# Matmul with RMS norm: the first pair of contraction tiles loaded through the software DMA queue, with its rows spread over the partitions

## Chip, cores and metric

The kernel runs on one core of one Trainium2 chip. The metric is the device time of one execution in microseconds. Before the change it is 222.75 us, the median of 7 runs (222.26 to 223.61). Work on the core is done by TensorE (matmuls and transposes; PE in the profile, its weight loads PEld), VectorE (DVE), ScalarE (ACT), GpSimd (POOL) and SyncE (SP). Loads and stores are issued by SP and ACT (two hardware queues) or by GpSimd (the software queue, which can also cast f32 to bf16 on the way), and all run on the core's 16 DMA engines.

## What is computed

```python
def setup_inputs():
    m, k, n = 2048, 2048, 2048
    return {
        "a": np.random.randn(m, k).astype(np.float32),
        "b": np.random.randn(k, n).astype(np.float32),
        "gamma": np.random.randn(n).astype(np.float32),
        "eps": np.float32(1e-5),
    }

def reference(a, b, gamma, eps):
    x = np.matmul(a, b)
    rms = np.sqrt(np.mean(x ** 2, axis=-1, keepdims=True) + eps)
    return (gamma * x / rms).astype(np.float32)
```

## The kernel before

A is cut into 16 blocks of 128 rows, the contraction into 16 tiles of 128 (KT), taken as 8 pairs (KP, index `kp`), and the columns of B into two halves (index `j`) of 1024, each two chunks of 512 (CH). TensorE needs both operands with the contraction on the partitions. B lies so in memory; A must be transposed. Whichever row of B lies on a partition, the same column of A must lie there in the transposed A: the order inside a contraction tile is free, as long as both agree.

**The head**, some 57 us, works while A and B stream in. The first four blocks of A (HB, 512 rows) are loaded pair by pair as pieces of 512 rows by 256 columns, and B's left half (j = 0) as tiles of 256 rows by 1024 columns, both cast to bf16 by the software queue (`load_head`, with the A load on L105 and the B load, `load_b`, on L99). TensorE transposes the A piece of the next pair (`transpose_head`, L172; VectorE moves the result to `head_at`, L177) and multiplies (`stream`, L384, seven accumulators in PSUM; the eighth group goes through `stream_in_parts`, L415, and VectorE's addition L421). Meanwhile VectorE forms sums and differences of quarters of B (`b_sums` L275, `b_sums_in_place` L280), since all later products use a two-by-two scheme with seven products instead of eight. Then B's right half (j = 1) streams in with its products for the first four blocks.

**The first pair** (kp = 0) goes another way, so as to start early. A's piece (512 rows by 256 columns, 0.5 MB) is loaded as f32 by SP (L91) into `a0f`, and B's two tiles of 128 rows by 1024 columns as f32 by ACT (L93) into `b0f`. `transpose_first` transposes A as f32 (L155), VectorE moves it to `head_at` as bf16 (L161), and VectorE and ScalarE cast B's halves into `raw[0][0]` (L158, L160). Until then TensorE runs eleven matmuls on zeros (L145) to keep its clock up. The identity for the transposes is made by GpSimd (a memset and a select), between its first and its second pair of loads, and VectorE casts it to bf16 and f16 (L138, L140).

**After the head** the other twelve blocks are taken in pairs (`group_half`, two halves each; `last_group` for the last pair). A block is loaded whole as f32 (two blocks by halves, L115, ten whole, L120), its row norms are taken on ScalarE (`row_norm`, L223), and `row_apply` scales the rows by a power of two and casts them to f16: on VectorE for blocks 4 and 5 (L244), on ScalarE for the others (L246). Blocks 4 and 5 are transposed on TensorE (`turn`, `transpose_half`, L189), the others by a DMA transpose from SP (L199). Sums of A's quarters (`a_sums`, L264), seven products (L289), and the combination on VectorE and ScalarE follow.

The order is written out by hand: `tc.manual_schedule()` puts each instruction on its engine's queue in the order of the program text, and every engine works its queue in that order. GpSimd's queue holds loads 1 to 3 of the pairs, the identity between them, small memsets, and then a load each time one that was issued eight loads earlier has landed.

The slots in SBUF that the change touches are parts of `early`:

```python
    a0f = early[:, 0:2048].bitcast(FP32).rearrange("p (r k) -> p r k", r=HB)
    b0f = [early[:, 2048 + t * 2048:2048 + (t + 1) * 2048].bitcast(FP32) for t in range(2)]
```

Of the kernel before, what the change touches and what calls it, by code (L numbers as in the profile page):

```python
# [8 lines left out]
FP32 = mybir.dt.float32  # L9
BF16 = mybir.dt.bfloat16  # L10
FP16 = mybir.dt.float16
I32 = mybir.dt.int32
ACTF = mybir.ActivationFunctionType
# [4 lines left out]
def kernel(  # L18
# [13 lines left out]
    nc = tc.nc  # L32
    P = 128
# [4 lines left out]
    W2 = 2 * P  # L38
    MB = M // P
    CH = 512  # L40
    NCH = N // CH
    HALF = N // 2
    HB = 4
# [15 lines left out]
    early = consts.tile([P, 6 * 2048], BF16, name="early")  # L59
    head_at = consts.tile([P, KT, HB, P], BF16, name="head_at")  # L60
    raw = [[consts.tile([P, 2, HALF], BF16, name=f"b_{j}_{kp}") for kp in range(KP)]
           for j in range(2)]
# [2 lines left out]
    sums = [t_left, t_right]  # L65

    a0f = early[:, 0:2048].bitcast(FP32).rearrange("p (r k) -> p r k", r=HB)
    b0f = [early[:, 2048 + t * 2048:2048 + (t + 1) * 2048].bitcast(FP32) for t in range(2)]
    NAH = 6
    ah_slot = [early[:, 6144 + s * 1024:6144 + (s + 1) * 1024].rearrange("p (r k) -> p r k", r=HB)  # L70
               for s in range(NAH)]
# [9 lines left out]
    def a16_slot(mb):  # L81
        flat = head_at.rearrange("p t r m -> p (t r m)").bitcast(FP16)
        return flat[:, (2 + mb % 2) * K:(3 + mb % 2) * K]
# [4 lines left out]
        return (at_even, at_odd)[(mb // 2) % 2][:, mb % 2]  # L88


    nc.sync.dma_start(out=a0f, in_=a[0:HB * P, 0:W2].rearrange("(r p) k -> p r k", p=P))  # L91
    for t in range(2):
        nc.scalar.dma_start(out=b0f[t], in_=b[t * P:(t + 1) * P, 0:HALF])  # L93

    def ah(kp):
        return ah_slot[(kp - 1) % NAH]

    def load_b(j, kp):
        nc.gpsimd.dma_start(  # L99
            out=raw[j][kp],  # L100
            in_=b[kp * W2:(kp + 1) * W2, j * HALF:(j + 1) * HALF].rearrange(
                "(t p) n -> p t n", p=P))

    def load_head(kp):
        nc.gpsimd.dma_start(  # L105
            out=ah(kp),
            in_=a[0:HB * P, kp * W2:(kp + 1) * W2].rearrange("(r p) k -> p r k", p=P))
        load_b(0, kp)

    a32 = {}  # L110
# [13 lines left out]
    def wait_for(src):  # L124

        nc.gpsimd.tensor_copy(out=pace, in_=src)

    load_head(1)
    identity_f = t_left[:, 2, KP - 1, 0:2 * P].bitcast(FP32)
    make_identity(nc, identity_f)  # L130
# [6 lines left out]
    identity = consts.tile([P, P], BF16, name="identity")  # L137
# [11 lines left out]

    def transpose_first():  # L150
        bank = [ps_t.tile([P, CH], FP32, name="tbank"), ps_a.tile([P, CH], FP32, name="acc")]
        view = [b.rearrange("p (r m) -> p r m", r=HB) for b in bank]
        for t in range(2):
            for r in range(HB):
                nc.tensor.matmul(view[t][:, r, :], a0f[:, r, t * P:(t + 1) * P], identity_f,  # L155
                                 is_transpose=True, start=(r == 0), stop=(r == HB - 1))
        for t in range(2):
            cast_first = [lambda: nc.vector.tensor_copy(out=raw[0][0][:, t, :CH],  # L158
                                                        in_=b0f[t][:, :CH]),
                          lambda: nc.scalar.copy(out=raw[0][0][:, t, CH:], in_=b0f[t][:, CH:])]  # L160
            move = [lambda h=h: nc.vector.tensor_copy(  # L161
                out=head_at[:, t, 2 * h:2 * h + 2, :], in_=view[t][:, 2 * h:2 * h + 2, :])
                for h in range(2)]
            for work in (cast_first + move if t == 0 else move + cast_first):
                work()

    def transpose_head(kp):
        bank = ps_t.tile([P, CH], FP32, name="tbank")
# [10 lines left out]
    a16 = {}  # L179
# [36 lines left out]
    factor = {}  # L216
# [22 lines left out]

    def row_apply(mb):  # L240
        a16[mb] = a16_slot(mb)
        if mb < HB + 2:

            nc.vector.tensor_scalar_mul(out=a16[mb], in0=a32.pop(mb), scalar1=factor.pop(mb))  # L244
        else:
            nc.scalar.activation(out=a16[mb], in_=a32.pop(mb), func=ACTF.Copy,  # L246
                                 scale=factor.pop(mb))


    def quarter(g, r, c):  # L250
# [141 lines left out]
    def load_later(n):  # L392
        for _ in range(min(n, len(later))):
            kind, which = later.pop(0)
            load_b(1, which) if kind == "b" else load_half(HB + which // 2, which % 2)
# [36 lines left out]
    for r in range(HB):  # L432
        x_tile(r, 0)
    early_sums = {4: ((2,), 0, 6), 5: ((5,), 0, 7), 6: ((1,), 0, KP)}
    transpose_first()
    for kp in range(KP):
        if kp + 4 < KP:
# [81 lines left out]
    row_factor(HB)  # L519
    product(PAIR, 1, 3, pair[5], start=False)  # L520
    row_apply(HB)
    nc.scalar.copy(out=x21, in_=pair[2])
    row_factor(HB + 1)
    row_apply(HB + 1)
    p7 = new_bank()
    turned = {}
# [88 lines left out]
    def hooks_of(g, j):  # L615
# [8 lines left out]
        def apply(mb):  # L624
            row_apply(mb)
            transpose_dma(mb)
# [204 lines left out]
```

## Time and profile before

| what | value |
|---|---|
| median of 7 runs | 222.75 us |
| the profiled execution, in all | 223.17 us |
| its span, first to last instruction | 221.4 us |
| TensorE busy | 208.9 us (94% of the span) |
| VectorE busy | 167.7 us (76%) |
| ScalarE busy | 128.3 us (58%) |
| GpSimd busy | 29.4 us (13%) |
| mean granted TensorE clock | 0.989 |
| read from HBM, written to it | 34.60 MB, 16.78 MB |
| first product on real data (L384) | 7.55 us |
| last B tile's first use | 56.85 us |

The profile is one execution taken by the hardware profiler. A row of the busy shares has 40 slices of 5.5 us, each digit the share in tenths. The chain of work that ended last is followed back from the last instruction, at each step to what released it. In a timeline line stand the start, the duration, the engine, the line of the program, the operation, what it writes and reads, and in brackets how long the engine had been idle before it and what ended that. "Time to landing" of a DMA runs from its issue to its completion as the engines see it. Rates of DMA count the bytes written, so a load that casts f32 to bf16 reads twice what the rate says.

### The profile page before, as it was taken

The page shows a single profiled execution, that of the slowest core. Times are in us where ns is not written, and L with a number is a line of the kernel's source. Part 1 is how long each engine was busy: PE and PEld are TensorE (multiplying, and loading weights), DVE is VectorE, ACT ScalarE, POOL GpSimd, SP SyncE. Part 2 cuts the span into 40 slices and gives each one's busy share as a digit, 9 for nine tenths or more (in the row PEclk, how much of TensorE's full clock was granted, in tenths as well). Part 3 has the DMA queues.
Part 4 walks back from the last instruction along what each step waited for, and adds up shares of the span by engine and source line. Part 5 has one row for each costly group of instructions (what it writes and reads, how often), then busy time and mean ns, then how long its engine had stood idle before and what let it go on. Part 6 is the DMA issues. An engine that isn't in the chain of part 4 may idle for free.

```text
span 221.4 us, 3002 instructions
## 1 busy us (share of the span) xinstructions
PE 208.9 (94%) x1015; PEld 97.7 (44%) x1035; DVE 167.7 (76%) x330; ACT 128.3 (58%) x263; POOL 29.4 (13%) x59
## 2 busy tenths in 40 slices
PE   7899999999999999999999999999999999999950
PEld 2445444444455444444444444444444444444430
DVE  2428889999988898989695639855794759797691
ACT  3110002920598898778845997399738995334580
POOL 7634232210000001200200002000200000000040
PEclk9999999999999999999999999999999999999995
DMA  6999999999938496947899049955798349044045
GB/s 185 226 201 209 204 207 211 212 210 241 421 111 355 181 298 110 372 184 203 213 313 406 16 88 267 369 219 95 183 298 374 69 90 380 33 189 192 1 191 189
DMA packets 36320, 47.13 MB, mean 213 GB/s; under 512 B 21968, under 2 KB 26064, under 8 KB 34896
## 3 DMA queue, kind: packets, MB, share of 16 engines
q0 software_dynamic: 9936, 23.33, 41.3%
q1 hardware_dynamic: 25936, 22.29, 33.4%
q10 hardware_dynamic: 432, 1.31, 1.9%
q8 instruction: 8, 0.13, 0.2%
q14 instruction: 8, 0.07, 0.1%
HBM read 34.60 MB, written 16.78 MB: 232 GB/s over the span
## 4 chain that ended last, share of the span: by engine, by line
PE 68%; DMA 23%; DVE 2%; POOL 2%; issue 2%; ACT 1%; DVEq 0%; ACTq 0%; POOLq 0%
PE acc L289 66%; DMA b<-in_b_dram 23%; POOL early L105 1%; DVE x L709 1%; PE acc L384 1%; POOL b L99 1%; DVE x L712 1%; ACT sq L307 0%; PE tbank L189 0%; PE acc L189 0%; DVE a L709 0%; ACT sq L778 0%; DVE x L786 0%; DVEq L826 0%; DVE x L790 0%
## 5 line engine op out<-in xcount | busy, mean ns | idle before, releaser
L289 PE MATMUL acc<-b,s 128*128 128x512 bf16 x397 | 91.5, 379 | 1.1 <-DMA b<-in_b_dram 0.5
L289 PEld LDWEIGHTS <-s 128*128 128x128 f16 (+1 forms) x512 | 49.9, 98 | 60.6 <-issue 0.8
L384 PE MATMUL acc<-b,head_at 128*128 128x512 bf16 x171 | 41.3, 379 | 0.7 <-DMA b<-in_b_dram 0.4
L307 ACT ACTIVATE sq<-x 128x512 bf16<-128x512 f32 x54 | 34.1, 632 | 6.9 <-DVE x L709 3.0
L366 DVE SCALAR_TENSOR_TENSOR x<-x,r,gamma_sb 128x1024 f32<-128x1024 f32 x28 | 34.8, 1281 | 0.7
L223 ACT ACTIVATE sq<-a 128x1024 bf16<-128x1024 f32 x24 | 25.3, 1055 | 1.8 <-DMA a<-in_a_dram 1.4
L384 PEld LDWEIGHTS <-head_at 128*128 128x128 bf16 x176 | 16.8, 98 | 20.2 <-issue 1.4
L246 ACT ACTIVATE head_at<-a,s 128x2048 f16<-128x2048 f32 x10 | 20.0, 1999 | 3.7 <-DVE s L233 3.7
L426 ACT COPY x<-acc 128x512 f32<-128x512 f32 x6 | 3.4, 588 | 25.1 <-PE acc L384 25.1
L289 PEld LDWEIGHTS <-head_at 128*128 128x128 f16 (+1 forms) x112 | 11.0, 98 | 13.2
L289 PE MATMUL acc<-early,head_at 128*128 128x512 bf16 x63 | 14.4, 379 | 0.1
L289 PEld LDWEIGHTS <-at_even 128*128 128x128 f16 x96 | 9.4, 98 | 11.3
L289 PE MATMUL acc<-early,s 128*128 128x512 bf16 x55 | 14.2, 379 | 0.0
L264 DVE TENSOR_TENSOR s<-head_at 128x1024 f16<-128x1024 f16 (+5 forms) x22 | 13.4, 638 | 0.1
L596 DVE TENSOR_TENSOR x<-x,x 128x512 f32<-128x512 f32 x9 | 6.2, 693 | 8.8 <-ACT x L594 8.3
L99 POOL DMA_DIRECT2D b<-in_b_dram x15 | 10.6, 707 | 15.4 <-DMA b<-in_b_dram 12.9
L578 ACT COPY x<-acc 128x512 f32<-128x512 f32 x9 | 5.2, 574 | 11.5 <-PE acc L289 11.5
L289 PE MATMUL acc<-t_left,s 128*128 128x512 bf16 x47 | 11.3, 379 | 0.1
L280 DVE TENSOR_TENSOR b<-b 128x1024 bf16<-128x1024 bf16 x16 | 10.9, 693 | 0.2
L289 PE MATMUL acc<-early,at_even 128*128 128x512 bf16 x48 | 10.8, 379 | 0.1
L289 PE MATMUL acc<-t_left,head_at 128*128 128x512 bf16 x48 | 10.8, 379 | 0.0
L289 PE MATMUL acc<-t_left,at_even 128*128 128x512 bf16 x47 | 10.8, 379 | 0.1
(111 smaller groups left out, 217.1 us busy)
## 6 DMA issues: line engine op xcount, KB each, us to landing
out_dram<-x SPq DMA_DIRECT2D x30, 512.0 KB, 3.8
a<-in_a_dram POOLq DMA_DIRECT2D x10, 1024.0 KB, 8.3
b<-in_b_dram POOLq DMA_DIRECT2D x15, 512.0 KB, 17.0
a<-in_a_dram POOLq DMA_DIRECT2D x4, 512.0 KB, 17.6
early<-in_a_dram POOLq DMA_DIRECT2D x7, 256.0 KB, 14.6
early<-in_b_dram ACTq DMA_DIRECT2D x2, 512.0 KB, 5.9
gamma_sb<-in_gamma_dram POOLq DMA_DIRECT2D x1, 1024.0 KB, 15.4
early<-in_a_dram SPq DMA_DIRECT2D x1, 512.0 KB, 5.5
```

Of the source, the lines that this page charges most:

```text
L99: nc.gpsimd.dma_start(out=raw[j][kp], in_=b[kp * W2:(kp + 1) * W2, j * HALF:(j + 1) * HALF].rearrange("(t p) n -> p t n", p=P))
L223: nc.scalar.activation(out=junk, in_=a32[mb][:, h * HALF:(h + 1) * HALF], func=ACTF.Square, scale=2.0 ** -8, accum_out=n2[:, h:h + 1])
L246: nc.scalar.activation(out=a16[mb], in_=a32.pop(mb), func=ACTF.Copy, scale=factor.pop(mb))
L264: nc.vector.tensor_tensor(out=sum_of(g, s)[:, lo:hi, :], in0=x[:, lo:hi, :], in1=y[:, lo:hi, :], op=op)
L280: nc.vector.tensor_tensor(out=flat[:, 1:3, :], in0=flat[:, 1:3, :], in1=flat[:, 0::3, :], op=ALU.add)
L289: nc.tensor.matmul(bank, lhsT[:, kp, :], rhs, start=(start and kp == 0), stop=(kp == KP - 1), skip_group_check=not start)
L307: nc.scalar.activation(out=sq[:, 0:CH], in_=src, func=ACTF.Square, scale=inv_sqrt_n, accum_out=msq[mb][:, c:c + 1])
L366: nc.vector.scalar_tensor_tensor(out=x, in0=x, scalar=inverse_of[mb], in1=gamma_sb[:, h * HALF:(h + 1) * HALF], op0=ALU.mult, op1=ALU.mult)
L384: nc.tensor.matmul(bank, head_at[:, kt, r, :], head_rhs(c, kt), start=(kt == 0), stop=(kt == KT - 1))
L426: copy(out=x_chunk(*g), in_=banks[g])
L578: nc.scalar.copy(out=c, in_=one[1])
L596: nc.vector.tensor_tensor(out=t, in0=t, in1=x12, op=ALU.add)
```

## The change

The first pair of contraction tiles is loaded, laid out and transposed in another way:

- B's rows of the first pair come by the software queue, cast to bf16 on the way and straight into `raw[j][0]`, as two loads of 128 rows for each half j (`load_first_pair`). For j = 0 they are the queue's first two loads. Row 32 v + u of a tile goes to partition 4 u + v, so neighbouring partitions hold rows 32 apart.
- A's 512-row piece of that pair is loaded by halves of 256 rows, one from SP and one from ACT.
- A's columns of that pair have to be permuted alike. VectorE and ScalarE cast two 128-row blocks each from `a0f` to a bf16 copy `a0`, reading with a stride of 32 elements; TensorE transposes the copy in bf16, and each of the two engines moves its half to `head_at`.
- For the blocks after the head, `row_apply` writes the first 256 columns permuted and the other 1792 as before: two instructions where there was one.
- Casts of B by VectorE and ScalarE and the f32 transposes go.

```diff
-    b0f = [early[:, 2048 + t * 2048:2048 + (t + 1) * 2048].bitcast(FP32) for t in range(2)]
+    a0 = early[:, 2048:3072].rearrange("p (r k) -> p r k", r=HB)
...
-    nc.sync.dma_start(out=a0f, in_=a[0:HB * P, 0:W2].rearrange("(r p) k -> p r k", p=P))
-    for t in range(2):
-        nc.scalar.dma_start(out=b0f[t], in_=b[t * P:(t + 1) * P, 0:HALF])
+    def spread_columns(cols):
+        return cols.rearrange("p (t v u) -> p t u v", v=4, u=P // 4)
+
+    def load_first_pair(j, t):
+        nc.gpsimd.dma_start(
+            out=raw[j][0][:, t, :],
+            in_=b[t * P:(t + 1) * P, j * HALF:(j + 1) * HALF].rearrange("(v u) n -> u v n", v=4))
+
+    for h, queue in enumerate((nc.sync, nc.scalar)):
+        queue.dma_start(out=a0f[:, 2 * h:2 * h + 2, :],
+                        in_=a[2 * h * P:(2 * h + 2) * P, 0:W2].rearrange("(r p) k -> p r k", p=P))
...
     def load_b(j, kp):
+        if kp == 0:
+            for t in range(2):
+                load_first_pair(j, t)
+            return
...
+    for t in range(2):
+        load_first_pair(0, t)
     load_head(1)
...
     def transpose_first():
         bank = [ps_t.tile([P, CH], FP32, name="tbank"), ps_a.tile([P, CH], FP32, name="acc")]
-        view = [b.rearrange("p (r m) -> p r m", r=HB) for b in bank]
-        for t in range(2):
-            for r in range(HB):
-                nc.tensor.matmul(view[t][:, r, :], a0f[:, r, t * P:(t + 1) * P], identity_f,
-                                 is_transpose=True, start=(r == 0), stop=(r == HB - 1))
-        for t in range(2):
-            cast_first = [lambda: nc.vector.tensor_copy(out=raw[0][0][:, t, :CH],
-                                                        in_=b0f[t][:, :CH]),
-                          lambda: nc.scalar.copy(out=raw[0][0][:, t, CH:], in_=b0f[t][:, CH:])]
-            move = [lambda h=h: nc.vector.tensor_copy(
-                out=head_at[:, t, 2 * h:2 * h + 2, :], in_=view[t][:, 2 * h:2 * h + 2, :])
-                for h in range(2)]
-            for work in (cast_first + move if t == 0 else move + cast_first):
-                work()
+        copies = (nc.vector.tensor_copy, nc.scalar.copy)
+        for h, copy in enumerate(copies):
+            for r in (2 * h, 2 * h + 1):
+                copy(out=a0[:, r, :].rearrange("p (t u v) -> p t u v", v=4, u=P // 4),
+                     in_=spread_columns(a0f[:, r, :]))
+        for h, copy in enumerate(copies):
+            view = bank[h].bitcast(BF16)[:, 0:CH].rearrange("p (t r m) -> p t r m", t=2, r=2)
+            for t in range(2):
+                for r in range(2):
+                    nc.tensor.matmul(view[:, t, r, :], a0[:, 2 * h + r, t * P:(t + 1) * P],
+                                     identity, is_transpose=True,
+                                     start=(t == 0 and r == 0), stop=(t == 1 and r == 1))
+            copy(out=head_at[:, 0:2, 2 * h:2 * h + 2, :], in_=view)
...
-        if mb < HB + 2:
-            nc.vector.tensor_scalar_mul(out=a16[mb], in0=a32.pop(mb), scalar1=factor.pop(mb))
-        else:
-            nc.scalar.activation(out=a16[mb], in_=a32.pop(mb), func=ACTF.Copy,
-                                 scale=factor.pop(mb))
+        x, s = a32.pop(mb), factor.pop(mb)
+        first = a16[mb][:, 0:W2].rearrange("p (t u v) -> p t u v", v=4, u=P // 4)
+        for dst, src in ((first, spread_columns(x[:, 0:W2])), (a16[mb][:, W2:], x[:, W2:])):
+            if mb < HB + 2:
+                nc.vector.tensor_scalar_mul(out=dst, in0=src, scalar1=s)
+            else:
+                nc.scalar.activation(out=dst, in_=src, func=ACTF.Copy, scale=s)
```

## The prediction, made before the changed kernel was built

> **What bounds the kernel now.** I read the page first: busy shares by slice, then the chain of work that ended last.
>
> ```profile
> PE   7899999999999999999999999999999999999950
> DMA  6999999999938496947899049955798349044045
> PE 68%; DMA 23%; DVE 2%; POOL 2%; issue 2%; ACT 1%; DVEq 0%; ACTq 0%; POOLq 0%
> PE acc L289 66%; DMA b<-in_b_dram 23%; POOL early L105 1%; DVE x L709 1%; PE acc L384 1%; POOL b L99 1%; DVE x L712 1%; ACT sq L307 0%; PE tbank L189 0%; PE acc L189 0%; DVE a L709 0%; ACT sq L778 0%; DVE x L786 0%; DVEq L826 0%; DVE x L790 0%
> ```
>
> TensorE looks full everywhere, but the chain says that up to about 57 us it is the loads of B (23% of the span) that end last, and after that matmuls in one unbroken run. The list of TensorE's waits up to 62 us shows how thin the difference is:
>
> ```profile
> PE acc L289 <- DMA b<-in_b_dram: 0.5, 1, 0.5
> PE acc L384 <- DMA b<-in_b_dram: 0.4, 1, 0.4
> PE tbank L415 <- DVE head_at L177: 0.3, 1, 0.3
> ```
>
> TensorE waits 0.4 us for a B tile at 24.5 us and 0.5 us for the last one at 56.85 us. So in the head two streams run side by side at one speed. The change works on the first 8 us of both; what counts is when the last B tile lands, and this follows from how early the software queue's stream gets going. The timeline of GpSimd gives its pace, because from its ninth load on GpSimd issues one load each time an older one lands:
>
> ```profile
> 1.25 0.94 POOL L105 DMA_DIRECT2D early<-in_a_dram  x1 [0.80 <-POOLq L812]
> 12.53 0.70 POOL L99 DMA_DIRECT2D b<-in_b_dram  x1 [1.76 <-DMA b<-in_b_dram]
> 16.32 0.70 POOL L99 DMA_DIRECT2D b<-in_b_dram  x1 [1.72 <-DMA b<-in_b_dram]
> 36.26 0.70 POOL L99 DMA_DIRECT2D b<-in_b_dram  x1 [1.76 <-DMA b<-in_b_dram]
> 38.73 0.57 POOL L115 DMA_DIRECT2D a<-in_a_dram  x1 [1.78 <-DMA b<-in_b_dram]
> 41.22 0.54 POOL L115 DMA_DIRECT2D a<-in_a_dram  x1 [1.92 <-DMA b<-in_b_dram]
> ```
>
> From 12.53 to 36.26 us six pairs (A tile 0.5 MB, B tile 1 MB) pass: 3.95 us a pair. 38.73 to 41.22 is one B tile: 2.5 us, which leaves 1.45 us for an A tile. The first B tile of this queue (issued at 2.18, time to landing 10.1 us) lands at 12.28 us. Taking off 2.5 and 1.45, the stream runs as if it had started at full pace at 8.32 us, though its first load was issued at 1.25 us. The windows show what filled the gap (columns: window, its length, busy time of PE, PEld, DVE, ACT, POOL, granted clock, DMA share, GB/s written):
>
> ```profile
> 2.50:3.00 0.50, 0.50 (x2) 0.15 (x1) 0.00 (x0) 0.49 (x2) 0.50 (x2) 1.00 0.86 176
> 4.00:4.50 0.50, 0.50 (x3) 0.22 (x2) 0.00 (x0) 0.00 (x0) 0.50 (x2) 1.00 1.01 383
> 6.00:6.50 0.50, 0.10 (x1) 0.13 (x2) 0.00 (x0) 0.00 (x0) 0.50 (x6) 1.00 0.78 214
> 8.00:8.50 0.50, 0.50 (x4) 0.26 (x3) 0.49 (x2) 0.00 (x0) 0.10 (x1) 1.00 1.42 203
> ```
>
> 383 GB/s written is f32 copied as f32 by the two hardware queues; about 205 at a share over 1.1 is the casting stream (it reads twice what it writes), and it reaches that only at 8 us. The three hardware loads land at 5.1 (B rows 0-127), 6.2 (A) and 8.7 us (B rows 128-255).
>
> **The change, part by part.** (1) *Bytes.* B's first pair (1 MB) goes from the ACT queue to the head of the software queue; A's 0.5 MB is split between SP and ACT. The new stream needs 2.5 + 1.45 + 2.5 = 6.45 us up to the landing of that same B tile. If it gets to full pace at S, the tile lands at S + 6.45, against 12.28: **break-even is S = 5.83 us**. Everything behind is the same stream at the same pace, so the last B tile moves by as much.
>
> How early can S be? No row shows this queue starting with little beside it at the beginning of the program, so I bound it. Early end: a 1 MB load of this queue that met idle DMA (L120, issued at 86.57) took 5.3 us to land; 2.5 of that is the stream, so 2.8 is start-up and S = 1.25 + 2.8 = 4.05. Late end: the queue needs the first 6.0 to 6.5 us whatever lies beside it, and S is 6.4. Which is nearer? The same 1 MB load took 8.4, 8.2 and 8.3 us at 109.6, 134.6 and 158.7 us, where SP's stores and transposes were running: 3 us more, so hardware-queue work ahead does hold this queue's start back. The first A load of the queue, 0.5 MB beside 1.5 MB of hardware loads, took 8.5 us. In the windows the casting stream appears when A's load is over (6.2 us). With 0.5 MB on the hardware queues, A is over earlier: 0.03 MB by 2.0 us, 0.27 MB by 3.5 us at the rates of those windows, the rest at 380 GB/s by 4.1 us, 0.4 us later for the landing. I take S = 4.7 (A's end, and a little to ramp up): the tile lands at 11.15, **1.1 us earlier**. Bounds: 1.8 us earlier (S 4.05) to 0.6 us later (S 6.4).
>
> A rule speaks against this. The Trainium skill, "DMA: Bandwidth & Descriptors", section "Issuing engines are not separate DMA queues", says that loads from all issuing engines share the same 16 DMA engines and interleave, and that issuing from another one saves only sequencer time. By the rule the bytes are as many as before and this part would be worth about nothing; the 8.3 against 5.3 us above do not look like even interleaving, and I go by them.
>
> (2) *GpSimd's issues.* Two more loads now stand ahead of the identity. 128-row loads cost 0.53 to 0.57 (L115), 256-row ones 0.70; I take 0.55 each, and 0.18 for the first of all (0.94 against 0.76 later). L105 and L99 then end at about 4.0 us, memset and select (0.6) at 4.6, DVE's two casts (0.23 + 0.22) at 5.05 instead of 3.9. A fourth extra issue (j = 1 is split as well) is hidden by GpSimd's waits of 1.5 us before each issue.
>
> (3) *First transposes.* Off go eight f32 transposes, four moves and four casts of B (0.62 on ACT twice, 0.75 and 0.43 on DVE); in come four strided casts 128x256, eight bf16 transposes, two moves. A 128x256 cast on DVE lies between 0.29 (from 0.43 for 512 and 0.23 for 128) and 0.42 (L161): two end at 5.65 to 5.9. Four transposes 0.4, a move 0.42 to 0.69: first matmul at **6.6 to 7.0** instead of 7.55, B's rows having landed at 4.7 + 1.25 = 5.95. ACT's half is used four matmuls (0.86 us) later and has 0.6-us rows of that size: hidden.
>
> ```profile
> 5.16 0.75 DVE L158 CAST b<-early 128x512 bf16<-128x512 f32 x1 [1.28 <-DMA early<-in_b_dram]
> 8.70 0.43 DVE L158 CAST b<-early 128x512 bf16<-128x512 f32 x1 [0.22 <-DMA early<-in_b_dram]
> ```
>
> The same cast took 0.75 us beside a GpSimd load issue and 0.43 beside none; the two new DVE casts lie beside issues, so up to 0.6 us may come on top: start at 7.0 to 7.5. The Trainium skill, "SBUF — State Buffer", section "SBUF: two separate sides", has it as an exclusive lock of a port that VectorE shares with GpSimd, under which software loads wait for their descriptors; by it S too would slip by the casts' 0.6 us, to 5.3.
>
> TensorE idles 1.6 us between 6.4 and 57 (50.6 less 49.0 busy), so with its start 0.5 us earlier it could be 2.0 us ahead at the end: the stream decides, and 1.1 us passes. VectorE runs without a gap from 36.6 to 56.6; the wait that begins this run is for TensorE's partial sum (L415), so it moves along.
>
> (4) *Row scaling in two pieces.* L244 (VectorE, two blocks): 1.28 for 2048 elements and 0.48 for 512 (L790) make 0.215 + 0.52 ns an element; 1792 + 256 cost 1.15 + 0.35 = 1.50, up to 1.58 if the strided piece goes at half speed: **0.2 to 0.3 us more**. This lies on the path: TensorE's block transposes wait for it,
>
> ```profile
> 62.66 1.29 DVE L244 TENSOR_SCALAR head_at<-a,s 128x2048 f16<-128x2048 f32 x1
> 64.00 0.45 PEld L189 LDWEIGHTS <-head_at 128*128 128x128 f16 x8 [0.36 <-DVE head_at L244]
> ```
>
> and matmuls follow without a break. The second block ends 0.95 us before its transposes: hidden. L246 (ACT, ten blocks): 2.00 becomes 1.77 + 0.42 (L778 shows 0.42 for 256): 0.2 each, hidden, since after 70 us no matmul waits for anything and the transposed block is in SBUF 4 us before its sums (85.9 against 89.96); without that cover, 2 us.
>
> **Sum.** -1.1 + 0.2 = **-0.9 us**: span 221.4 to 220.5; that execution took 223.17 in all, 0.42 over the median of 222.75. From the median: **221.85**. Its own range: -1.8 + 0.2 gives 221.15, and a gain of 0.6 in the stream 222.35.
>
> **Rivals.**
> A. *The software queue starts no earlier* (slower). Its first bytes come at 6.0 to 6.5 us because the program's first software load needs 5 us, not because of its neighbours; the first B rows then land last. For it: first issue at 1.25, nothing before 6; no row has the queue starting early in the program. Against: 2.8 us of start-up at 86.57. Price: S = 6.4 costs 0.6, a start-up ramp up to 0.6 more, row scaling 0.2: +0.8 to +1.4, **223.8**. It decides from S = 5.6 on (5.83 less the 0.2).
> B. *Even sharing.* The queues share the engines, as the rule above says; total bytes unchanged, S near 5.5; TensorE starts earlier and waits longer at 24 and 56 us. Stream -0.3, scaling +0.2: **222.65**, no change. For it: DMA share is 1.0 already from 3.5 us. Against: the 3 us above.
> C. *Spread rows read faster as well.* 176 GB/s at 2.5 us rises to 383 later; if the order of rows causes that and the spread mends it, B's first pair gains up to 0.7 us besides: stream -1.8, total -1.6, **221.15**, at the limit of TensorE's start. Against: the same low rate could be any start.
>
> **Chances.** Forecast 0.42, C 0.08, A 0.30, B 0.20. About 0.3% (0.67 us) is what this measurement tells from no change: faster means under 222.1, slower over 223.4. Forecast and C give faster 0.50 (a little of the forecast's range reaches into B's, and B's into it); same 0.20; slower 0.30. The range for 8 in 10: from 220.9 (C and some) to 223.9 (the middle of A).
>
> **What would show it.** Right: the POOL timeline's first B tile of the pair loop landing near 11.2, first L384 matmul near 6.8, the last DMA wait of TensorE near 55.8, L244 as two rows of 1.15 and 0.35. A: a casting rate only from 6.4 us, the first matmul after 8. B: an early first matmul and waits for B over 1 us later. Wrong altogether: a wait of TensorE after 70 us, from ACT's longer scaling.

## The result: slower

The changed kernel takes **225.09 us** (median of 12 runs, 223.99 to 226.09) against 222.74 us (31 runs), a ratio of 1.011, 95% interval 1.0095 to 1.0125. The forecast was 221.85 with a range of 220.9 to 223.9. The profiled execution took 225.77 us with a span of 224.0, 2.6 more than the span before. In this and all later medians and ratios, executions more than 1.5% above the fastest of their kernel, which ran at a lower clock, are left out.

First the page of the changed kernel: TensorE by slice, then the chain that ended last, by engine and by line. L304, L399, L237 and L262 are here what L289, L384, L223 and L246 were.

```profile
PE   7889999999899999999999998999999999999950
PE 12%; ACT 6%; DVE 5%; issue 2%; DVEq 0%; ACTq 0%
PE acc L304 12%; ACT head_at L262 2%; ACT sq L237 2%; DVE s L279 1%; ACT sq L322 1%; DVE x L724 1%; DVE x L727 1%; DVE x L611 0%; DVE a L724 0%; DVE x L620 0%; DVE x L606 0%; DVE x L601 0%; ACT norm L240 0%; ACT sq L793 0%; DVE x L801 0%
```

The loads of B are gone from the shares. The chain now leaves TensorE at 184.8 us and runs back through ScalarE: its row scaling (`head_at` L262) and its row norms (L237) stand in it. The list of TensorE's waits says the same:

```profile
PE acc L304 <- ACT x L593: 1.7, 3, 0.7
PE acc L160 <- DVE pace L150: 1.5, 1, 1.5
PE acc L399 <- DMA b<-in_b_dram: 1.2, 3, 0.5
PE acc L304 <- DMA b<-in_b_dram: 0.9, 1, 0.9
```

Three waits for a copy of ScalarE (L593) make 1.7 us; there were none after 70 us before. The waits for B tiles grew from 0.9 to 2.1 us.

Set side by side, the same matmul starts 0.96 us *earlier* at the first product (6.59 against 7.55), 0.09 later once the second pair's B tile has come (12.37 against 12.28), 0.46 later at the last B tile (57.31 against 56.85), 0.41 later when the groups begin, and then the distance grows by 0.6 at 110 us, 0.7 at 135, 0.2 at 160 and 0.7 at 184, to 2.58 at the last matmul. So of 2.6 us the groups made 2.2 and the head 0.4. The head's part is no more than executions differ by: three of the runs below leave the head as it was before, and in their profiles the last B tile is first used at 56.15, 56.41 and 56.84 us.

### The profile page after: what moved, and what is told of

Its sections match the earlier page's. It is cut to its first block, busy times and chain, and to the rows that moved or that the text cites. A ratio compares the mean times of both kernels' runs of the same rounds, so it can differ in the third digit from the quotient of the medians.

```text
span 224.0 us, 3016 instructions
## 1 busy us (share of the span) xinstructions
PE 209.0 (93%) x1015; PEld 97.2 (43%) x1035; DVE 166.5 (74%) x329; ACT 132.7 (59%) x274; POOL 30.8 (14%) x62
## 5 line engine op out<-in xcount | busy, mean ns | idle before, releaser
L304 PE MATMUL acc<-b,s 128*128 128x512 bf16 x397 | 91.5, 379 | 1.5 <-DMA b<-in_b_dram 0.9
L304 PEld LDWEIGHTS <-s 128*128 128x128 f16 (+1 forms) x512 | 49.9, 98 | 61.0 <-issue 1.2
L399 PE MATMUL acc<-b,head_at 128*128 128x512 bf16 x171 | 41.3, 379 | 1.7 <-DMA b<-in_b_dram 1.2
L237 ACT ACTIVATE sq<-a 128x1024 bf16<-128x1024 f32 x24 | 25.3, 1054 | 4.3 <-DMA a<-in_a_dram 3.9
L262 ACT ACTIVATE head_at<-a,s 128x256 f16<-128x256 f32 (+1 forms) x20 | 24.2, 1261 | 2.9 <-DVE s L247 2.9
L399 PEld LDWEIGHTS <-head_at 128*128 128x128 bf16 x176 | 16.8, 98 | 21.1 <-issue 2.2
L304 PEld LDWEIGHTS <-head_at 128*128 128x128 f16 (+1 forms) x112 | 10.9, 98 | 14.0 <-issue 1.0
L304 PEld LDWEIGHTS <-at_even 128*128 128x128 f16 x96 | 9.4, 98 | 12.7 <-issue 1.6
L304 PE MATMUL acc<-early,head_at 128*128 128x512 bf16 x63 | 14.4, 379 | 0.5 <-ACT x L593 0.4
L304 PE MATMUL acc<-early,s 128*128 128x512 bf16 x55 | 14.2, 379 | 0.0
L593 ACT COPY x<-acc 128x512 f32<-128x512 f32 x9 | 5.1, 572 | 12.0 <-PE acc L304 7.7
L304 PE MATMUL acc<-early,at_even 128*128 128x512 bf16 x48 | 10.8, 379 | 1.3 <-ACT x L593 1.3
L112 POOL DMA_DIRECT2D b<-in_b_dram x14 | 9.9, 707 | 13.5 <-DMA b<-in_b_dram 11.6
L304 PE MATMUL acc<-t_left,s 128*128 128x512 bf16 x47 | 11.3, 379 | 0.1
L139 POOL COPY pace<-x 128x1 f32<-128x1 f32 x4 | 1.6, 412 | 67.4 <-DVE x L620 66.8
L245 DVE TENSOR_SCALAR s<-norm 128x1 f32<-128x1 f32 x12 | 1.8, 152 | 12.2 <-ACT norm L240 12.2
```

The lines of the kernel that those rows point to most:

```text
L112: nc.gpsimd.dma_start(out=raw[j][kp], in_=b[kp * W2:(kp + 1) * W2, j * HALF:(j + 1) * HALF].rearrange("(t p) n -> p t n", p=P))
L237: nc.scalar.activation(out=junk, in_=a32[mb][:, h * HALF:(h + 1) * HALF], func=ACTF.Square, scale=2.0 ** -8, accum_out=n2[:, h:h + 1])
L262: nc.scalar.activation(out=dst, in_=src, func=ACTF.Copy, scale=s)
L304: nc.tensor.matmul(bank, lhsT[:, kp, :], rhs, start=(start and kp == 0), stop=(kp == KP - 1), skip_group_check=not start)
L399: nc.tensor.matmul(bank, head_at[:, kt, r, :], head_rhs(c, kt), start=(kt == 0), stop=(kt == KT - 1))
L593: nc.scalar.copy(out=c, in_=one[1])
```

## Experiments

Each kernel was timed against the kernel before on the same chip. Intervals are of the ratio of times, 95%.

### Which part costs what

**Plain rows.** The changed kernel without any permutation:

```diff
-            in_=b[t * P:(t + 1) * P, j * HALF:(j + 1) * HALF].rearrange("(v u) n -> u v n", v=4))
+            in_=b[t * P:(t + 1) * P, j * HALF:(j + 1) * HALF])
...
-                copy(out=a0[:, r, :].rearrange("p (t u v) -> p t u v", v=4, u=P // 4),
-                     in_=spread_columns(a0f[:, r, :]))
+                copy(out=a0[:, r, :], in_=a0f[:, r, :])
```

and `row_apply` as in the kernel before.

> The changed kernel with B's first rows laid out in plain order, so without any permutation: A's copy is contiguous and the row scaling is one instruction a block again. Theory 1 (ScalarE's strided scaling costs the groups about 2.1 us, the head's loads 0.45 us): 223.2 us, no TensorE wait after 70 us. Theory 2 (the new order of loads costs the groups their time, the scaling does not): near 225. Theory 3 (rows 32 apart are slow to read, and that is why the stream gained nothing): the second 128-row load lands 1 us or more earlier and the kernel comes to 221.7 to 222.2.

**Scaling only**: the kernel before with the changed `row_apply`.

> The kernel before with only the row scaling in two pieces, the first one strided. Its output has A's first 256 columns permuted for blocks 4 to 15 and B's rows not, so these blocks are not the reference's. Theory 1: 224.6 us, TensorE waits for ScalarE's copies at 112, 135 and 186 us, 2 us in all. Theory 2: 222.8.

**Split, not strided**: the same, but the first piece is `(a16[mb][:, 0:W2], x[:, 0:W2])`.

> The kernel before with the row scaling in two contiguous pieces, 256 and 1792 columns. If the second instruction alone is what costs: 0.2 us a block on ScalarE (0.42 + 1.77 against 2.00), half of what the strided one costs; the slack of 1.35 us that ScalarE's copy has in the kernel before absorbs it: 222.8 to 223.1. If the stride is innocent: near 224.6, as with it.

**Head only**: the changed kernel with the old `row_apply`.

> The changed kernel with the row scaling of the kernel before, one instruction, not permuted, so blocks 4 to 15 miss the permutation of A's first 256 columns. Theory 1: 223.2 us, the whole difference to the kernel before made by 57 us. Theory 2: near 225.

| kernel | median, us | ratio to before (interval) |
|---|---|---|
| plain rows | 222.70 | 0.999 (0.9978 to 1.0003) |
| scaling only | 224.66 | 1.0087 (1.0061 to 1.0113) |
| split, not strided | 222.46 | 0.9998 (0.9989 to 1.0007) |
| head only | 222.78 | 1.0012 (1.0001 to 1.0023) |

Scaling alone brings 1.9 us, the head alone 0.0 to 0.5 (0.3 by the ratio): theory 1 holds for the groups, theory 2 falls. The 0.45 us that theory 1 gave to the head's loads is not borne out: plain rows and head only came to 222.70 and 222.78, not 223.2. Scaling in two pieces is free if neither is strided. Theory 3 is not borne out either: with plain rows the stream of loads is as slow as with spread ones (below).

### Is it the stride or the time?

ScalarE's groups by form (the mean of one in ns after the bar), first of the changed kernel, then of the one split without a stride:

```profile
L262 ACT ACTIVATE head_at<-a,s 128x1792 f16<-128x1792 f32 x10 | 17.8, 1777 | 0.0
L262 ACT ACTIVATE head_at<-a,s 128x256 f16<-128x256 f32 x10 | 7.4, 744 | 2.9 <-DVE s L247 2.9
```

```profile
L247 ACT ACTIVATE head_at<-a,s 128x1792 f16<-128x1792 f32 x10 | 17.7, 1773 | 0.0
L247 ACT ACTIVATE head_at<-a,s 128x256 f16<-128x256 f32 x10 | 5.0, 502 | 3.1 <-DVE s L233 3.1
```

The same 256 columns take 744 ns read with a step of 32 elements and 502 ns in a row. In the timeline both pieces together take 2.40 to 2.44 us strided, 2.19 contiguous and 2.00 as one instruction: 0.43 and 0.19 us more a block. To see whether the stride does anything else than cost time, the time was spent without it.

**Three contiguous pieces**, on the kernel before:

```diff
+        for dst, src in ((a16[mb][:, 0:P], x[:, 0:P]), (a16[mb][:, P:W2], x[:, P:W2]), (a16[mb][:, W2:], x[:, W2:])):
```

> The kernel before with the row scaling in three contiguous pieces of 128, 128 and 1792 columns, correct and without any stride. ScalarE then needs about 0.37 us more a block, nearly what the strided piece costs (0.43). If ScalarE's time a block is what counts, beyond a slack that 0.2 us did not use up: 1.0 to 1.8 us slower than the kernel before, 223.7 to 224.5, with TensorE waits for ScalarE's copies. If it takes a stride: 222.5, as with two contiguous pieces.

224.14 us (223.08 to 225.20), ratio 1.007 (1.0046 to 1.0094). A block took 2.37 us, 0.37 more. Three doses on one engine then: 0.19 us a block costs nothing, 0.37 costs 1.6 us, 0.43 costs 1.9 us. What counts is ScalarE's time beyond a slack (the time by which its work is done before another engine needs it), and the slack can be read from the kernel before, around 133 us: ScalarE's queue first, then TensorE's.

```profile
129.52 1.99 ACT L246 ACTIVATE head_at<-a,s 128x2048 f16<-128x2048 f32 x1
131.41 0.56 ACT L594 COPY x<-acc 128x512 f32<-128x512 f32 x1
132.01 0.63 ACT L307 ACTIVATE sq<-x 128x512 bf16<-128x512 f32 x1
132.64 0.57 ACT L578 COPY x<-acc 128x512 f32<-128x512 f32 x1
```

```profile
132.17 1.67 PE L289 MATMUL acc<-early,s 128*128 128x512 bf16 x7
133.90 2.32 PE L289 MATMUL acc<-early,at_even 128*128 128x512 bf16 x10
```

Every engine works its queue in order. The copy L578 takes the result of the half's first product out of its accumulator, into which the fourth product (here from 133.90 us) accumulates further; it must wait for the copy. The copy ended at 133.21, 0.69 us ahead; near 157 and 181 us it is 0.69 too, near 108 us 1.47 (the expectation above took 1.35). It has no gap before it: second block's scaling, copy, square, copy. In a group two blocks are scaled ahead of this copy, so 0.19 a block takes 0.38 of the 0.69 us, and 0.37 or 0.43 take 0.74 or 0.86. The changed kernel shows the cover gone:

```profile
131.43 2.40 ACT L262 ACTIVATE head_at<-a,s 128x256 f16<-128x256 f32 x2
133.74 0.57 ACT L609 COPY x<-acc 128x512 f32<-128x512 f32 x1
134.34 0.63 ACT L322 ACTIVATE sq<-x 128x512 bf16<-128x512 f32 x1
134.97 0.57 ACT L593 COPY x<-acc 128x512 f32<-128x512 f32 x1
```

```profile
135.58 1.67 PE L304 MATMUL acc<-early,at_even 128*128 128x512 bf16 x7 [0.72 <-ACT x L593]
```

The copy ends at 135.54, and TensorE, which had been idle for it, goes on at 135.58.

The subtraction alone gives a small part of the loss: 0.74 or 0.86 less 0.69 is 0.05 or 0.17 us a group. This is what the traces show where nothing else is late. From the start of the third product to that of the fourth there are 1.73 us in the kernel before, 1.80 with three pieces (132.27 to 134.07) and 1.91 with scaling only (132.74 to 134.65); in the changed kernel the growth of 0.2 at 160 us is of this kind. Three groups of it make 0.5 of the 2.2 us. The rest came from waits for DMA, which stand ahead of the copy in ScalarE's queue of the changed kernel:

```profile
94.29 1.06 ACT L237 ACTIVATE sq<-a 128x1024 bf16<-128x1024 f32 x1 [3.34 <-DMA a<-in_a_dram]
122.05 1.06 ACT L237 ACTIVATE sq<-a 128x1024 bf16<-128x1024 f32 x1 [0.52 <-DMA a<-in_a_dram]
169.32 0.58 ACT L593 COPY x<-acc 128x512 f32<-128x512 f32 x1 [4.35 <-DMA out_dram<-x]
```

Before the wait at 110 us the block's DMA transpose comes later, GpSimd waits for that before it issues the next block's load (87.67 against 86.57 us), the load takes 6.5 us to land instead of 5.3, and ScalarE's row norm waits 3.3 us for it instead of 1.4. (In "split, not strided" the load took 6.5 us as well and ScalarE waited 2.8, at no loss.) Before the one at 135 the row norm waits 0.5 us for a load, where it waited for none. Before the one at 184 a copy waits 4.35 us for the DMA of a store, where it waited 3.79 for TensorE. That the added time on ScalarE costs 1.9 us is shown by the runs; why these two transfers came so late was not followed.

**The strided piece on VectorE**, in the changed kernel, all blocks:

```diff
+        nc.vector.tensor_scalar_mul(out=first, in0=spread_columns(x[:, 0:W2]), scalar1=s)
```

and only the other 1792 columns on ScalarE.

> The changed kernel whole, but the strided 256 columns of each block's scaling go to VectorE, where the row for blocks 4 and 5 is 0.46 us, and ScalarE keeps the 1792 contiguous ones (1.78 against 2.00 before). Theory 1 (ScalarE's 0.4 us a block is the groups' loss): TensorE's waits for ScalarE's copies after 70 us go, 222.8 to 223.2. If permuting as such, or the second instruction, is what hurts: near 225 as the changed kernel.

A miss: 228.62 us, ratio 1.0289 (1.0256 to 1.0322). The waits of TensorE and of ScalarE (after 70 us) in that kernel:

```profile
PE acc L304 <- ACT x L593: 4.3, 1, 4.3
```

```profile
ACT sq L237 <- DMA a<-in_a_dram: 8.1, 1, 8.1
```

There is one wait of 4.3 us instead of three small ones, and it came by the way of the wait at 110 us. VectorE reaches its strided piece of the second block only at 83.70 us, behind its own queue; the transpose goes out at 84.24 instead of 82.83; GpSimd issues the two next loads 1.2 us apart, at 89.72 and 90.91; ScalarE's norm waits 8.1 us for its block; the copy that TensorE needs stands behind the norm. So less work on ScalarE did not help where the work that feeds its queue came later. The wait cost more than itself: TensorE's granted clock fell after it, to 0.50 from 103 to 105 us, and the next sixteen matmuls took 5.30 us where they took 3.62 before.

```profile
101.85 5.30 PE L304 MATMUL acc<-t_left,head_at 128*128 128x512 bf16 x16 [4.29 <-ACT x L593]
```

After it TensorE waits for nothing more, as theory 1 had it for a shorter scaling. So the run does not contradict the doses above, but as a cure it failed.

### Why the earlier stream gained nothing

The software queue did deliver earlier: its first load landed at 6.35 us (5.1 after the issue at 1.25; before, its first landed at 9.75). But it was slow. Windows of the changed kernel (columns as in the prediction; full pace is 205 to 214 GB/s written):

```profile
3.50:4.00 0.50, 0.50 (x3) 0.16 (x2) 0.00 (x0) 0.00 (x0) 0.50 (x2) 1.00 1.19 291
4.50:5.50 1.00, 1.00 (x6) 0.36 (x4) 0.92 (x4) 1.00 (x2) 1.00 (x3) 1.00 0.93 115
5.50:6.50 1.00, 0.75 (x9) 0.39 (x7) 0.56 (x2) 0.38 (x2) 1.00 (x2) 1.00 1.56 117
6.50:7.50 1.00, 0.91 (x5) 0.44 (x6) 0.03 (x1) 0.41 (x1) 1.00 (x6) 1.00 0.55 66
8.50:9.50 1.00, 0.98 (x5) 0.38 (x4) 0.00 (x0) 0.00 (x0) 0.70 (x1) 1.00 1.42 214
```

A's two hardware loads landed at 4.1 and 4.4 us, so the windows from 4.5 us show the software queue alone. From 4.5 to 7.5 us it moved half of what it can, 99 GB/s, and the second load of 128 rows landed at 8.5 us (6.5 after its issue). With 3 us at 99 instead of 208 GB/s, 1.6 us of stream are lost, and the gain with it. The DMA share over these 3 us is 1.01, against 1.22 from 8.5 to 11.5 us: the DMA engines were not much less busy, they moved less. Six kernels, all on the one with plain rows, looked for what slows it.

**Issues later**: GpSimd waits for the second load before it issues the second and third pair.

```diff
+    landed = consts.tile([P, 1], FP32, name="landed")
+    nc.gpsimd.tensor_copy(out=landed, in_=raw[0][0][:, 1, 0:1])
     for kp in range(2, 4):
         load_head(kp)
```

> On the kernel with plain rows: GpSimd waits for the second 128-row load of B before it issues the second and third pair, so it issues nothing between about 4.5 us and that landing. Theory I (GpSimd's own burst of issues slows the stream to a third of its pace from 4.5 to 7.5 us): the 128-row load lands at 6.2 to 6.5 instead of 8.0, the first tile of the next B pair near 11, the kernel comes to 221.7 to 222.2. Theory V (VectorE's casts beside it, the port they share) and theory W (the second load is slow whatever GpSimd does): it lands at 8 as before, the later loads start later, 222.7 to 223.5.

**A between**: the order is B rows 0-127, A, B rows 128-255, B.

> On the kernel with plain rows: the order of the first software loads is B rows 0-127, A's second piece, B rows 128-255, B's second tile. If the slow stretch belongs to the time from 4.5 to 7.5 us (theories I and V), A's piece crawls through it and lands as late as the 128-row load did, near 8, and B rows 128-255 then land at 9 or later at full pace. If it belongs to the second 128-row load itself (theory W), A's piece lands near 6.3 and the 128-row load needs its 3 us after that, until 9.5.

**Casts on ScalarE**: `nc.scalar.copy` in place of `copy` for A's four casts.

> On the kernel with plain rows: all four casts of A's first piece on ScalarE, so that VectorE runs only the two 128x128 casts of the identity beside GpSimd's issues from 4.5 to 6 us. Theory V: the second 128-row load lands before 7 and the stream gains 1 us. Theories I and W: it lands at 8 as before; the first product starts up to 0.4 us later for the longer chain of casts, and the total stays at 222.7.

**One load** of 256 rows for B's first pair.

> On the kernel with plain rows: B's first pair as one load of 256 rows, as for all other pairs, so one issue fewer on GpSimd and no second 128-row load. Theory W (a load of 128 rows that follows another is slow): the 1 MB lands near 6.5. Theories I and V: it lands near 8, as the second half did, the first product waits for it and starts 1.4 us later, and the total is 222.7 to 223.3.

**Late start**: `nc.vector.memset(early[:, 0:8192].bitcast(FP32), 0.0)` and a memset of two elements of `raw[0][0]` ahead of all loads.

> On the kernel with plain rows: two memsets on VectorE (about 4.3 us) stand ahead of every first load, so that all loads start some 4 us later. Theory W1 (the slow stretch belongs to the clock time since the program began, until about 8 us): the loads meet only its end, and the second 128-row load lands within 3.5 us of the first bytes of the queue, as the full pace gives. Theory W2 (it belongs to the beginning of the loads themselves, whatever the time): the same slow stretch appears 4 us later, between 8.5 and 12 us, and the second 128-row load lands at about 12. The total is about 226.5 (W2) or 225 (W1).

**Other rows**: `b[K - W2 + t * P:K - W2 + (t + 1) * P, ...]` for B's first pair.

> On the kernel with plain rows: B's first pair is read from the last 256 rows of B instead of the first (the product is not the reference's). If the slow stretch belongs to those first rows, the second 128-row load now lands before 6.8 us. If it belongs to the beginning of the loads, it lands at about 8 as before, with 100 to 140 GB/s written from 4.5 to 7.5 us.

| kernel | GB/s written, 4.5 to 7.5 us | second load landed, us | time, us (interval of the ratio) |
|---|---|---|---|
| changed kernel | 99 | 8.5 | 225.09 (1.0095 to 1.0125) |
| plain rows | 105 | 8.6 | 222.70 (0.9978 to 1.0003) |
| head only (spread rows) | 89 | 9.1 | 222.78 (1.0001 to 1.0023) |
| issues later | 115 | 8.8 | 223.80 (1.0038 to 1.0083) |
| A between | 129 | 8.4 (A's piece; B's rows 128-255 9.8) | 222.90 (1.0001 to 1.0022) |
| casts on ScalarE | 126 | 8.1 | 222.56 (0.9994 to 1.0029) |
| one load | 119 | 9.9 (the whole of it) | 224.33 (1.0036 to 1.0110) |
| other rows | 143 | 8.0 | 222.69, one run |
| late start | 112, from 8.5 to 11.5 us | 13.0 | 227.06, one run |

Each rate is from one profile. The changed kernel and "head only" have the same head and show 99 and 89, so a difference of 10 says nothing. In "one load" TensorE waited 3.9 us, until 10.0, and its granted clock fell to 0.50 from 9 to 15 us of the profiled execution: its first twelve matmuls took 5.28 us where they took 2.87 in the kernel before. So its time says little of the loads.

Each theory named a landing that did not come: I 6.2 to 6.5 us (8.8), V before 7 (8.1), W near 6.5 for the single load (9.9), the first rows before 6.8 (8.0). With A's piece in second place, that piece landed as late as the B load had. The windows of "issues later" and of "late start" decide most:

```profile
4.50:7.50 3.00, 2.91 (x14) 1.43 (x13) 1.19 (x5) 0.67 (x3) 0.04 (x1) 1.00 1.01 115
```

```profile
7.50:8.50 1.00, 1.00 (x4) 0.38 (x3) 0.00 (x0) 0.00 (x0) 0.93 (x3) 1.00 1.27 300
8.50:11.50 3.00, 2.70 (x17) 1.19 (x16) 1.39 (x5) 1.30 (x3) 3.00 (x5) 1.00 1.04 112
13.00:15.00 2.00, 1.71 (x14) 0.86 (x14) 0.00 (x0) 0.00 (x0) 0.96 (x2) 1.00 1.22 211
```

With GpSimd busy for 0.04 of 3 us the stretch was as slow (115), so its burst of issues is not the cause; what that kernel lost, it lost by issuing later. With all loads starting 4 us later the stretch came 4 us later as well: it belongs to the beginning of the loads and not to a time since the program began. Other rows, rows in another order, one load for two and VectorE's casts taken away changed it by 6 to 38 GB/s and did not end it; with A's 1 KB pieces in its place the rate was 129. So it is a start-up of this stream, some 7 us from its first issue to a lasting full pace (1.25 to 8.5 us in the changed kernel, 5.46 to 13 in "late start"); **what makes it stays open**. No run took away the hardware loads of A, which end as the stretch begins, so a part of theirs is not excluded. Something like it also comes later: in the changed kernel GpSimd's load issued at 87.67 us met idle DMA engines, and the windows show 66 and 82 GB/s from 88 to 90 us and 287 in the next.

## Why the prediction failed, step by step

**Step 1, the stream (-1.1 us), failed.** That the queue would deliver earlier with fewer hardware loads beside it came true: first landing at 6.35 against 9.75 us. What failed is full pace from S = 4.7 us on: it came at about 8.5. The second pair's B tile was first used at 12.37 us against 12.28; the stream's term measured **+0.1** instead of -1.1. Its premise was also read wrongly: the 1 MB loads that took 8.2 to 8.4 us had a second load issued 0.5 us behind them on the same queue, the one that took 5.3 had its next only 2.9 us behind, so the 3 us between them do not show what hardware loads do. The windows of the kernel before had shown a low stretch too, 214 to 221 GB/s from 6 to 7.5 us after 383; I put it down to the change from one queue to the other, and whether it is the same start-up is not shown.

**Steps 2 and 3 held.** VectorE's identity casts ended at 4.95 us (5.05 forecast), the first product came at 6.59 (6.6 to 7.0). As step 3 said, the head's end did not follow TensorE's start. (Two slips of the working changed nothing: splitting j = 1 adds a third issue and not a fourth, and step 4's own figures give 1.63, not 1.58, for a strided piece at half speed.) The two strided casts on VectorE took 0.44 us each, above the upper bound of 0.42; nothing waited for them beyond that. The Trainium skill, "SBUF — State Buffer", section "SBUF: two separate sides", has VectorE and GpSimd exclude each other at a shared port, which holds up the descriptors of software loads. With VectorE's casts of A on ScalarE the rate went from 105 to 126 GB/s, far from 208, so these casts explain at most a little of the slow stretch here.

**Step 4, scaling, was the larger failure: the sentence "hidden, since after 70 us no matmul waits for anything".** First the size: the row for 256 contiguous elements (0.42) was taken for a strided read; it took 0.74, and a block 0.43 us more instead of 0.2 (0.19 without the stride). Then the cover: that nothing waits says that the slack is not negative, not how long it is. I measured the slack of the transposed block (4 us), not that of what is queued behind the scaling on ScalarE, the copy that frees TensorE's accumulator: 0.69 us for two scalings. The sign that I had named for "wrong altogether", a wait of TensorE after 70 us from ScalarE's longer scaling, is the one that came. That the price I named for a lost cover, 2 us, is near what was paid (1.9 alone, 2.2 in the trace) is luck: it was ten blocks at 0.2 us with no cover at all, and it was ten at 0.43 with part of the cover left, and waits for DMA besides. On VectorE the size was right (1.52, forecast 1.50 to 1.58), but it cost TensorE nothing: TensorE's block transposes were 0.42 us late, no more than the head's end already was.

**The rivals.** A had the right sign and the wrong mechanism: the queue did not start late, and a stream that gained nothing costs 0.0 to 0.5 us, not 1.4. B's "no gain from the stream" is near what the head did, without even sharing being the reason shown. None of them had the groups in it. C, a gain by the order of the rows, falls with the runs of plain rows.

## What to carry over

A wait of zero does not price a longer instruction: for each one made longer, find the next instruction on the same engine that another engine waits for, and subtract their times; here 0.69 us stood against two instructions 0.43 longer each. The difference is only the least price: ask also which loads and stores are issued later for it, and who waits for those; here that made the larger part. And a queue's pace in full flow says little of its first microseconds: read the start-up from the trace's own start, in short windows.

## What the runs showed of the hardware

- ScalarE read 256 f32 elements a partition with a step of 32 elements in 744 ns and in a row in 502 ns (f16 out); VectorE's strided scaling of the same size took 456 to 464 ns.
- The software queue's first loads ran at 89 to 143 GB/s written from 4.5 to 7.5 us (full: 205 to 214) in the eight kernels of the table that issue them at 1.25 us, and at 112 from 8.5 to 11.5 us when the loads began 4 us later.
- After 4.3 and 3.9 us without a matmul (VectorE's strided piece, one load) TensorE's granted clock fell to 0.50 for some microseconds; after 1.7 us (A between) it stayed at 1.00.
